# Scaled rotary embedding: the 0/1 matrix built small and repeated by VectorE, fills moved to GpSimd, PSUM copies in pairs

One core of one Trainium2 chip. The metric is the device time of one execution in microseconds (us), the median of several; lower is better. All inputs and the output are in HBM.

## The reference

```python
# x: (8, 8, 1024, 64) float32; freqs: (32,); positions: (1024,); scale = 0.5
angles = np.outer(positions * scale, freqs)
cos, sin = np.cos(angles), np.sin(angles)
x_first, x_second = x[..., :32], x[..., 32:]
out_first  = x_first * cos - x_second * sin
out_second = x_first * sin + x_second * cos
```

The tables depend on the position alone and are shared by the 64 (batch, head) pairs. x and the result are 16.78 MB each.

## The kernel before

Four sets (u = 0 to 3) of 16 heads. A partition holds 128 consecutive positions of one head, so the tables `T` differ between partitions. They are computed once, eight positions per partition (`tab`), and spread by 16 matmuls with a 0/1 matrix `sel`; each result goes from PSUM to the fp16 tile `T` by a copy. GpSimd's queue loads x and converts it to fp16 on the way; half of set 0 comes as fp32 on two other queues and is converted by ScalarE.

```python
    pin(nc.sync.dma_start(out=X0f[:, :Q], in_=xv[0][:, NH : NH + Q]))
    ...                                           # positions, freqs, rest of X0f on ScalarE's queue
    pin(nc.gpsimd.dma_start(out=Xf[0][:, :NH], in_=xv[0][:, :NH]))
    pin(nc.gpsimd.memset(sel, 0.0))               # 128 x 2048
    pin(nc.gpsimd.dma_start(out=Xf[1], in_=xv[1]))
    pin(nc.gpsimd.affine_select(out=sel, ...))    # 128 x 2048
    for u in range(2, NU):
        pin(nc.gpsimd.dma_start(out=Xf[u], in_=xv[u]))
    ...                                           # two fills on VectorE
    pin(nc.vector.tensor_copy(out=posf, in_=...)) # 8 positions, int32 -> fp32 (L98)
    ...                                           # y = posf * cfreq, range reduction, two Sin -> tab
    for g in range(G):                            # 16 matmuls and copies; VectorE has g = 0, 2, 4, 6
        ...
    pin(nc.scalar.copy(out=Xf[0][:, NH:], in_=X0f[:, :NH]))
    for u in range(NU):
        OUT = xout.tile([P, N], FP32, tag="O")
        for s in range(2):
            ...                                   # four VectorE instructions, 7.0 us in all
            pin(nc.scalar.copy(out=OUT[:, ns], in_=Xf[u][:, ns]))      # fp16 -> fp32, 3.6 us
            if u >= NU // 2:
                pin(nc.sync.dma_start(out=ov[u][:, ns], in_=OUT[:, ns]))
        if u < NU // 2:
            pin(nc.gpsimd.dma_start(out=ov[u], in_=OUT))
```

Of the kernel before, what the change touches and what calls it, by code (L numbers as in the profile page):

```python
# [10 lines left out]
FP32 = mybir.dt.float32  # L11
FP16 = mybir.dt.float16
I32 = mybir.dt.int32
AF = mybir.ActivationFunctionType
ALU = mybir.AluOpType
# [6 lines left out]
def kernel(  # L22
# [8 lines left out]
    nc = tc.nc  # L31
    pin = tc.keep_in_program_order
# [3 lines left out]
    half = D // 2  # L36
    P = nc.NUM_PARTITIONS
    HEADS = 16
    HP = P // HEADS
    K = S // HP  # L40
    N = K * D
    NU = NBH // HEADS
    KH = K // 2
    NH = KH * D
    K8 = S // P
    G = P // HP
    W = K8 * half
    assert S % HP == 0 and D == 2 * half and NBH % HEADS == 0 and G * K8 == K

    fscale = float(scale)  # L50

    xv = x.rearrange("b h s d -> (b h s d)").rearrange("(u p n) -> u p n", p=P, n=N)
    ov = out.rearrange("b h s d -> (b h s d)").rearrange("(u p n) -> u p n", p=P, n=N)

    consts = ctx.enter_context(tc.tile_pool(name="consts", bufs=1))
    tmp = ctx.enter_context(tc.tile_pool(name="tmp", bufs=1))
    psum = ctx.enter_context(tc.tile_pool(name="psum", bufs=1, space=bass.MemoryType.PSUM))
    spread = ctx.enter_context(tc.tile_pool(name="spread", bufs=6, space=bass.MemoryType.PSUM))
    xin = ctx.enter_context(tc.tile_pool(name="xin", bufs=1))
    xout = ctx.enter_context(tc.tile_pool(name="xout", bufs=3))  # L60

# [13 lines left out]
    Xf = [t.rearrange("p k h j -> p (k h j)") for t in X]  # L75


    sel = consts.tile([P, G, HEADS, HP], FP16)
    pin(nc.gpsimd.dma_start(out=Xf[0][:, :NH], in_=xv[0][:, :NH]))  # L79
    pin(nc.gpsimd.memset(sel, 0.0))  # L80
    pin(nc.gpsimd.dma_start(out=Xf[1], in_=xv[1]))  # L81
    pin(nc.gpsimd.affine_select(  # L82
        out=sel, in_=sel, compare_op=ALU.not_equal, fill=1.0, base=0,
        pattern=[[-1, G], [0, HEADS], [-G, HP]], channel_multiplier=1,
    ))
    for u in range(2, NU):
        pin(nc.gpsimd.dma_start(out=Xf[u], in_=xv[u]))  # L87


    coef = consts.tile([1, P], FP32)  # L90
    pin(nc.vector.memset(coef, fscale / (2.0 * np.pi)))  # L91
    quarter = consts.tile([P, 1], FP32)
    pin(nc.vector.memset(quarter, np.pi / 2.0))
    cfreq = psum.tile([P, half], FP32)
    nc.tensor.matmul(out=cfreq, lhsT=coef, rhs=freq_row, start=True, stop=True)  # L95

# [2 lines left out]
        out=posf, in_=pos_i64.bitcast(I32).rearrange("p (k t) -> p k t", t=2)[:, :, 0]  # L99
# [3 lines left out]
        out=y,  # L103
# [8 lines left out]
        out=r, in0=m, scalar=_MAGIC, in1=y, op0=ALU.subtract, op1=ALU.subtract  # L112
    ))
    tab = consts.tile([P, 2, K8, half], FP16)
# [3 lines left out]
        out=ra.bitcast(I32), in0=r.bitcast(I32), scalar1=0x7FFFFFFF, scalar2=None, op0=ALU.bitwise_and  # L118
# [2 lines left out]


    T = consts.tile([P, 2, K, half], FP16)
    for g in range(G):
        ps = spread.tile([P, 2, K8, half], FP32, tag="g")
        nc.tensor.matmul(  # L126
            out=ps.rearrange("p t k j -> p (t k j)"),
            lhsT=sel[:, g].rearrange("s h q -> s (h q)"),
            rhs=tab.rearrange("s t k j -> s (t k j)"),
            start=True, stop=True,  # L130
        )
        dst = T[:, :, g * K8 : (g + 1) * K8, :]
        if g % 2 == 0 and g < G // 2:
            pin(nc.vector.tensor_copy(out=dst, in_=ps))  # L134
        else:
            pin(nc.scalar.copy(out=dst, in_=ps))  # L136
# [3 lines left out]
# [3 lines that stand above are left out]
# [9 lines left out]
                out=Xs[:, :, 0, :], in0=Xs[:, :, 0, :], in1=pr[:, :, 1, :], op=ALU.subtract  # L152
            ))
            pin(nc.vector.tensor_tensor(  # L154
                out=Xs[:, :, 1, :], in0=pr[:, :, 0, :], in1=Xs[:, :, 1, :], op=ALU.add
# [41 lines left out]
```

## Time and profile before

| | before |
|---|---|
| time, median of 3 | 85.02 us (84.86 to 85.13) |
| profiled execution | 84.89 us; its profiled span, first to last instruction, 82.7 us |
| VectorE / ScalarE / GpSimd busy | 75% / 49% / 11% |

Head of the page: the span, then busy us, share of the span and number of instructions of each engine.

```profile
span 82.7 us, 185 instructions
PE 6.0 (7%) x18; PEld 2.5 (3%) x18; DVE 62.4 (75%) x43; ACT 40.6 (49%) x24; POOL 9.1 (11%) x12
```

VectorE is the busiest compute engine and the change takes work off it. The four stores on the sync queue (issue duration and first and last start; then the times from issue to landing; the later a store is issued, the shorter its time):

```profile
L159 SPq DMA_DIRECT2D out_dram<-OUT x4: 332/332/342, 53.8 to 75.0; - x4
DMA to landing us min/median/max: 6.8/10.1/13.4
```

The last store is issued at 75.0 us and lands 6.8 us later.

### The profile page before, as it was taken

What the parts mean: (1) busy time and instruction counts of PE and PEld (TensorE: products, weight loads), DVE (VectorE), ACT (ScalarE), POOL (GpSimd) and SP (SyncE); (2) the same over time, 40 slices, a digit from 0 to 9 for tenths busy, and PEclk for the clock granted to TensorE, in tenths of its full rate; (3) what the DMA queues carried; (4) which work ended last, traced back from release to release, by engine and by line L of the source; (5) the groups of instructions that cost most, each with busy time, mean ns of one, the idle gap of its engine ahead of it and who ended that gap; (6) DMA issues with size and microseconds to landing.
All of it is one profiled execution on the core that took longest, in us unless ns stands there. A gap on an engine that the chain in (4) does not pass through costs nothing.

```text
span 82.7 us, 185 instructions
## 1 busy us (share of the span) xinstructions
PE 6.0 (7%) x18; PEld 2.5 (3%) x18; DVE 62.4 (75%) x43; ACT 40.6 (49%) x24; POOL 9.1 (11%) x12
## 2 busy tenths in 40 slices
PE   0011099600000000000000000000000000000000
PEld 0010033100000000000000000000000000000000
DVE  0029657999899999999999999999999999400000
ACT  0600337999993098059219607903940880492000
POOL 4999400000000000200000200000000000000000
PEclk9999999999555555555555555555555555555555
DMA  3899997997998899799989989998999999999991
GB/s 51 327 319 269 301 341 170 254 254 151 230 254 190 190 254 238 158 238 254 127 349 412 507 364 428 475 460 357 420 436 412 428 444 412 452 420 436 436 412 55
DMA packets 1874, 26.22 MB, mean 317 GB/s; under 512 B 338, under 2 KB 338, under 8 KB 338
## 3 DMA queue, kind: packets, MB, share of 16 engines
q0 software_dynamic: 864, 15.73, 66.3%
q1 hardware_dynamic: 720, 9.44, 27.3%
q10 hardware_dynamic: 290, 1.06, 3.2%
HBM read 16.79 MB, written 16.78 MB: 406 GB/s over the span
## 4 chain that ended last, share of the span: by engine, by line
DVE 58%; ACT 15%; DMA 6%; issue 5%; PE 4%; DVEq 1%; ACTq 0%
DVE pr L149 19%; DVE X L150 19%; DVE X L154 9%; DVE X L151 6%; DMA pos_i<-in_positions_dram 6%; ACT T L136 5%; ACT OUT L157 4%; PE ps L126 4%; ACT X L137 4%; DVE posf L98 3%; DVEq L192 1%; DVE r L111 1%; DVE y L102 1%; ACT tab L120 1%; ACT tab L115 1%
## 5 line engine op out<-in xcount | busy, mean ns | idle before, releaser
L157 ACT CAST OUT<-X 128x4096 f32<-128x4096 f16 x8 | 28.9, 3616 | 24.2 <-DVE X L154 24.2
L149 DVE TENSOR_TENSOR pr<-X,T 128x4096 f16<-128x4096 f16 x8 | 18.3, 2292 | 0.9 <-ACT X L137 0.4
L150 DVE TENSOR_TENSOR X<-X,T 128x4096 f16<-128x4096 f16 x8 | 18.3, 2292 | 0.3
L151 DVE TENSOR_TENSOR X<-X,pr 128x2048 f16<-128x2048 f16 x8 | 9.8, 1224 | 0.3
L154 DVE TENSOR_TENSOR X<-pr,X 128x2048 f16<-128x2048 f16 x8 | 9.7, 1218 | 0.0
L136 ACT CAST T<-ps 128x512 f16<-128x512 f32 x12 | 6.3, 621 | 1.9 <-PE ps L126 1.9
L98 DVE CAST posf<-pos_i 128x8 f32<-128x8 int32 x1 | 2.5, 2496 | 4.7 <-DMA pos_i<-in_positions_dram 4.7
L126 PE MATMUL ps<-tab,sel 128*128 128x512 f16 x16 | 5.4, 500 | 4.1 <-ACT tab L120 4.0
L161 POOL DMA_DIRECT2D out_dram<-OUT x2 | 1.1, 534 | 37.3 <-ACT OUT L157 37.3
L134 DVE CAST T<-ps 128x512 f16<-128x512 f32 x4 | 2.8, 691 | 1.7 <-PE ps L126 1.7
L82 POOL TENSOR_SCALAR_AFFINE_SELECT sel<-sel 128x2048 f16<-128x2048 f16 x1 | 3.9, 3865 | 0.1
L137 ACT CAST X<-X0f 128x4096 f16<-128x4096 f32 x1 | 3.7, 3704 | 0.0
L115 ACT ACTIVATE tab<-r 128x256 f16<-128x256 f32 x1 | 0.4, 416 | 6.1 <-DVE r L111 6.1
L115 ACT ACT_TABLE_LOAD x1 | 1.3, 1283 | 2.1 <-issue 2.1
L126 PEld LDWEIGHTS <-sel 128*128 128x128 f16 x16 | 2.0, 122 | 6.9 <-issue 4.3
L80 POOL MEMSET sel<- 128x2048 f16 x1 | 1.8, 1823 | 0.0
L87 POOL DMA_DIRECT2D X<-in_x_dram x2 | 1.1, 554 | 0.0
L95 PE MATMUL cfreq<-freq_row,coef 1*128 1x32 f32 x2 | 0.6, 392 | 5.9 <-DMA freq_row<-in_freqs_dram 5.9
L91 DVE MEMSET coef<- 1x128 f32 x1 | 0.2, 165 | 0.8 <-PEq L178 0.8
L79 POOL DMA_DIRECT2D X<-in_x_dram x1 | 0.7, 667 | 0.8 <-POOLq L178 0.8
L95 PEld LDWEIGHTS cfreq<-freq_row,coef 1*128 1x128 f32 x2 | 0.5, 306 | 5.8 <-issue 5.8
L81 POOL DMA_DIRECT2D X<-in_x_dram x1 | 0.5, 542 | 0.0
(10 smaller groups left out, 2.4 us busy)
## 6 DMA issues: line engine op xcount, KB each, us to landing
out_dram<-OUT POOLq DMA_DIRECT2D x2, 4096.0 KB, 18.7
out_dram<-OUT SPq DMA_DIRECT2D x4, 2048.0 KB, 10.1
X<-in_x_dram POOLq DMA_DIRECT2D x3, 2048.0 KB, 24.1
X0f<-in_x_dram SPq DMA_DIRECT2D x1, 1024.0 KB, 4.8
X<-in_x_dram POOLq DMA_DIRECT2D x1, 1024.0 KB, 11.6
X0f<-in_x_dram ACTq DMA_DIRECT2D x1, 1024.0 KB, 13.1
pos_i<-in_positions_dram ACTq DMA_DIRECT2D x1, 8.0 KB, 4.9
freq_row<-in_freqs_dram ACTq DMA_DIRECT2D x1, 0.1 KB
```

The lines of the kernel that those rows point to most:

```text
L82: pin(nc.gpsimd.affine_select(out=sel, in_=sel, compare_op=ALU.not_equal, fill=1.0, base=0, pattern=[[-1, G], [0, HEADS], [-G, HP]], chann ...
L98: pin(nc.vector.tensor_copy(out=posf, in_=pos_i64.bitcast(I32).rearrange("p (k t) -> p k t", t=2)[:, :, 0]))
L115: pin(nc.scalar.activation(out=tab[:, 0], in_=r, func=AF.Sin, bias=0.0, scale=-_TWO_PI_DN))
L126: nc.tensor.matmul(out=ps.rearrange("p t k j -> p (t k j)"), lhsT=sel[:, g].rearrange("s h q -> s (h q)"), rhs=tab.rearrange("s t k j -> s ...
L134: pin(nc.vector.tensor_copy(out=dst, in_=ps))
L136: pin(nc.scalar.copy(out=dst, in_=ps))
L137: pin(nc.scalar.copy(out=Xf[0][:, NH:], in_=X0f[:, :NH]))
L149: pin(nc.vector.tensor_tensor(out=pr, in0=Xs, in1=sin_b, op=ALU.mult))
L150: pin(nc.vector.tensor_tensor(out=Xs, in0=Xs, in1=cos_b, op=ALU.mult))
L151: pin(nc.vector.tensor_tensor(out=Xs[:, :, 0, :], in0=Xs[:, :, 0, :], in1=pr[:, :, 1, :], op=ALU.subtract))
L154: pin(nc.vector.tensor_tensor(out=Xs[:, :, 1, :], in0=pr[:, :, 0, :], in1=Xs[:, :, 1, :], op=ALU.add))
L157: pin(nc.scalar.copy(out=OUT[:, ns], in_=Xf[u][:, ns]))
```

## The change

Its intent is to relieve VectorE: VectorE's four PSUM copies become two of double size (and ScalarE's twelve become six), two fills go to GpSimd, and GpSimd builds a 128-column matrix in place of 2048 columns, which one VectorE copy repeats.

```diff
--- before.py
+++ after.py
@@ -55,7 +55,7 @@
     consts = ctx.enter_context(tc.tile_pool(name="consts", bufs=1))
     tmp = ctx.enter_context(tc.tile_pool(name="tmp", bufs=1))
     psum = ctx.enter_context(tc.tile_pool(name="psum", bufs=1, space=bass.MemoryType.PSUM))
-    spread = ctx.enter_context(tc.tile_pool(name="spread", bufs=6, space=bass.MemoryType.PSUM))
+    spread = ctx.enter_context(tc.tile_pool(name="spread", bufs=3, space=bass.MemoryType.PSUM))
     xin = ctx.enter_context(tc.tile_pool(name="xin", bufs=1))
     xout = ctx.enter_context(tc.tile_pool(name="xout", bufs=3))
 
@@ -75,22 +75,24 @@
     Xf = [t.rearrange("p k h j -> p (k h j)") for t in X]
 
 
+
+    one = consts.tile([P, G, HP], FP16)
     sel = consts.tile([P, G, HEADS, HP], FP16)
+    coef = consts.tile([1, P], FP32)
+    quarter = consts.tile([P, 1], FP32)
     pin(nc.gpsimd.dma_start(out=Xf[0][:, :NH], in_=xv[0][:, :NH]))
-    pin(nc.gpsimd.memset(sel, 0.0))
-    pin(nc.gpsimd.dma_start(out=Xf[1], in_=xv[1]))
+    pin(nc.gpsimd.memset(coef, fscale / (2.0 * np.pi)))
+    pin(nc.gpsimd.memset(quarter, np.pi / 2.0))
+    pin(nc.gpsimd.memset(one, 0.0))
     pin(nc.gpsimd.affine_select(
-        out=sel, in_=sel, compare_op=ALU.not_equal, fill=1.0, base=0,
-        pattern=[[-1, G], [0, HEADS], [-G, HP]], channel_multiplier=1,
+        out=one, in_=one, compare_op=ALU.not_equal, fill=1.0, base=0,
+        pattern=[[-1, G], [-G, HP]], channel_multiplier=1,
     ))
-    for u in range(2, NU):
+    for u in range(1, NU):
         pin(nc.gpsimd.dma_start(out=Xf[u], in_=xv[u]))
 
 
-    coef = consts.tile([1, P], FP32)
-    pin(nc.vector.memset(coef, fscale / (2.0 * np.pi)))
-    quarter = consts.tile([P, 1], FP32)
-    pin(nc.vector.memset(quarter, np.pi / 2.0))
+    pin(nc.vector.tensor_copy(out=sel, in_=one.unsqueeze(2).broadcast_to((P, G, HEADS, HP))))
     cfreq = psum.tile([P, half], FP32)
     nc.tensor.matmul(out=cfreq, lhsT=coef, rhs=freq_row, start=True, stop=True)
 
@@ -121,16 +123,17 @@
 
 
     T = consts.tile([P, 2, K, half], FP16)
-    for g in range(G):
-        ps = spread.tile([P, 2, K8, half], FP32, tag="g")
-        nc.tensor.matmul(
-            out=ps.rearrange("p t k j -> p (t k j)"),
-            lhsT=sel[:, g].rearrange("s h q -> s (h q)"),
-            rhs=tab.rearrange("s t k j -> s (t k j)"),
-            start=True, stop=True,
-        )
-        dst = T[:, :, g * K8 : (g + 1) * K8, :]
-        if g % 2 == 0 and g < G // 2:
+    for g in range(0, G, 2):
+        ps = spread.tile([P, 2, 2, W], FP32, tag="g")
+        for i in range(2):
+            nc.tensor.matmul(
+                out=ps[:, i].rearrange("p t w -> p (t w)"),
+                lhsT=sel[:, g + i].rearrange("s h q -> s (h q)"),
+                rhs=tab.rearrange("s t k j -> s (t k j)"),
+                start=True, stop=True,
+            )
+        dst = T[:, :, g * K8 : (g + 2) * K8, :].rearrange("p t (i k) j -> p i t (k j)", i=2)
+        if g in (0, 4):
             pin(nc.vector.tensor_copy(out=dst, in_=ps))
         else:
             pin(nc.scalar.copy(out=dst, in_=ps))
```

## The prediction

> **What bounds the kernel now.** I first read section 4 of the page, the chain that ended last, because the change is aimed at VectorE. It names VectorE with 58%, and its pieces in order of time show VectorE running from 14.6 us to 71.3 us with one gap of 0.4 us. That suggests VectorE bounds the kernel. I don't think so, and the reason is in sections 2 and 3 and in the window table.
>
> Section 2 and 3 of the page:
>
> ```profile
> DMA  3899997997998899799989989998999999999991
> q0 software_dynamic: 864, 15.73, 66.3%
> q1 hardware_dynamic: 720, 9.44, 27.3%
> q10 hardware_dynamic: 290, 1.06, 3.2%
> HBM read 16.79 MB, written 16.78 MB: 406 GB/s over the span
> ```
>
> The three queues add up to 96.8% of the time of the 16 DMA engines, and they are busy in the first half (loading x) as well as in the second (storing the result). Nothing is read twice: 8 x 8 x 1024 x 64 floats are 16.78 MB each way, so there is no traffic to save.
>
> Windows cut at the landings (issue time plus time to landing; X1 22.6, X2 32.2; the first half of X0 at 12.9); the last columns are the DMA share and GB/s:
>
> ```profile
> 22.60:32.20 9.60, 0.00 (x0) 0.00 (x0) 9.46 (x6) 5.96 (x2) 0.00 (x0) 0.50 1.02 218
> 42.30:81.00 38.70, 0.00 (x0) 0.00 (x0) 28.61 (x17) 18.03 (x5) 0.53 (x1) 0.50 0.99 428
> 81.00:82.70 1.70, 0.00 (x0) 0.00 (x0) 0.00 (x0) 0.00 (x0) 0.00 (x0) 0.50 0.00 0
> ```
>
> The loads convert fp32 to fp16 and GB/s counts the fp16 bytes, so 218 is 436 GB/s on the HBM side. The stores run from 42.3 to 81.0 at 428 GB/s with share 0.99; 16.78 MB in 38.7 us are 434 GB/s. Both phases run at about the same rate, near 435, and the DMA engines do not pause between them. All stores wait behind the X3 load: the first result (4.19 MB) is issued at 33.0 us, yet by the byte rates its data begins only when X3 is in, at about 42.3.
>
> Does the last store come late enough to set the end? It is issued at 75.0 us (the last ScalarE conversion ends at 74.95). Before it 7 x 2.097 = 14.68 MB are queued; between 42.3 and 75.0, 32.7 x 0.434 = 14.18 MB have gone. So 0.50 MB is left, 1.15 us of work. The first load on that same queue was issued at 0.74 us and its first bytes moved between 1.5 and 2.0, so the issue takes about 1 us to take effect. The backlog just covers this. **Two limits end together**: VectorE's chain feeds the last store just as the DMA queue would have run dry. Making only one of them faster gains almost nothing; making VectorE slower by more than some tenths costs directly.
>
> **What VectorE's start waits for.** The timeline at the start (start, duration):
>
> ```profile
> 4.29 3.87 POOL L82 TENSOR_SCALAR_AFFINE_SELECT sel<-sel 128x2048 f16<-128x2048 f16 x1
> 5.69 2.50 DVE L98 CAST posf<-pos_i 128x8 f32<-128x8 int32 x1 [4.69 <-DMA pos_i<-in_positions_dram]
> 5.86 0.60 PE L95 MATMUL cfreq<-freq_row,coef 1*128 1x32 f32 x2 [5.86 <-DMA freq_row<-in_freqs_dram]
> 8.29 0.42 DVE L102 TENSOR_TENSOR y<-posf,cfreq 128x256 f32<-128x256 f32 x1
> 10.43 5.56 PE L126 MATMUL ps<-tab,sel 128*128 128x512 f16 x16 [3.96 <-ACT tab L120]
> 13.99 4.50 ACT L136 CAST T<-ps 128x512 f16<-128x512 f32 x9 [0.23 <-PE ps L126]
> 14.61 2.29 DVE L149 TENSOR_TENSOR pr<-X,T 128x4096 f16<-128x4096 f16 x1 [0.31 <-ACT T L136]
> ```
>
> A cast of 8 elements takes 2.50 us and ends at 8.19, just after GpSimd's affine_select (8.16). It is not working, it is locked out.
>
> **The Trainium skill.** (1) "SBUF — State Buffer", section "Who interferes with whom": GpSimd and a VectorE copy or cast in a two-port mode take one shared port pair exclusively, and the later one blocks wholly. The pair of lines above agrees (ends 0.03 us apart). (2) "VectorE: DVE Perf Modes", "The perf-mode tier table": a 2048-element 16-bit SBUF copy in 4x mode takes 693 ns, and PSUM sources lose the two-port modes. The trace has no such copy; its PSUM copies (512 fp32, 691 ns) fit one element per cycle plus 151 cycles at that page's 0.96 GHz. (3) "ScalarE: Activation LUTs", "What ACT_TABLE_LOAD costs": 0.833 ns per element plus a fixed part, partly overlapped back to back. The trace agrees: eight copies of 512 from 14.57 to 18.49 are 0.49 us each, 0.43 + 0.06. (4) "DMA: Bandwidth & Descriptors", "Where 436 GB/s comes from": 435.2 GB/s is the ceiling of the 16 ports. The 434 and 436 above agree, so no reserve is left in the DMA rate.
>
> **The change, part by part.**
>
> *Small matrix on GpSimd.* Removed: a fill of 2048 columns (1.82 us) and an affine_select of 2048 (3.87 us). Added: the two fills from VectorE (about 0.1 each, by the 128x1 fills of the trace), a fill of 128 columns (about 0.2) and an affine_select of 128 columns (3.87/16 = 0.24 plus a fixed part that I put at 0.2 to 0.3). The first load's issue ends at 1.93 as before, so the small matrix is there at about 3.0. Then three load issues of 0.55 us, done near 4.7. They now come before 8.1 us, but they queue behind X0, which moves until about 12.9: no byte moves sooner.
>
> *The repeating copy on VectorE.* 0.69 us in 4x mode; runs of 8 elements and the repeated axis could bring it to 1.2 or 2.3 us, both estimates from (2). It starts at 3.0 and ends between 3.7 and 5.3, before the positions land at 5.67. Hidden. TensorE needs the matrix only when tab is there.
>
> *The cast freed.* It starts at 5.69 and takes about 0.16 us, as the 1x128 fill does (0.165). Now y waits for cfreq, which ends at 5.86 + 0.60 = 6.46; with the 0.10 us that lay ahead of y before, y starts at about 6.55 instead of 8.29, **-1.74 us**. From y to the first spread matmul nothing changes (10.43 - 8.29 = 2.14), so that one starts at 8.69.
>
> *Copies in pairs.* The first eight matmuls come 0.43 us apart, and the copies follow them, so here a larger grain costs: the last copy of the first half holds 1024 elements and takes 0.58 + 0.43 = 1.01 us instead of 0.58. It starts as before, 3.56 us after the first matmul. On VectorE 2 x 1.22 = 2.45 replaces 4 x 0.69 = 2.76, all while it waits for TensorE. The three buffers hold: the fourth pair needs the first, free about 2.3 us after the first matmul, and begins at 2.6. So pr starts 4.18 + 0.45 = 4.63 after it: at 13.3 instead of 14.61, **-1.3 us**. X0's first half lands at about 12.9, so the margin there shrinks from 1.7 to 0.4 us. On ScalarE the second half of T takes 4 x 0.92 = 3.7 instead of 3.9; the conversion of X0's second half ends about 1.4 us earlier, near 20.6, and VectorE's first half ends at 13.3 + 7.02 = 20.3. It waits 0.3 instead of 0.4 us. From there VectorE is about 1.4 us ahead.
>
> *Sum on VectorE:* the last multiply chain ends near 69.9 instead of 71.3, the last store is issued near 73.6 instead of 75.0. **Sum at the end:** by 73.6 us 13.58 of the 14.68 MB have gone; 1.10 MB, 2.5 us, is queued ahead of the last store. Its data begins when it did before, at 76.1, and ends at 76.1 + 2.097/0.434 = 80.9. The 1.4 us turn into a longer wait in the queue. I predict **84.8 us** (85.02 before; 0.2 for small gaps near the end that a longer queue may fill).
>
> **Rivals.**
> 1. VectorE's chain sets the end after all, and the 1.4 us come through: 83.6. For it: the chain of section 4. Against it: the stores start only at 42.3, and 16.78 MB need 38.6 us at the rate seen. Even this would be 1.6%.
> 2. The load phase gets shorter, as GpSimd's descriptor work is done early. 16.79 MB took from about 1.7 to 42.3; at 435 GB/s they need 38.6, so 2.0 us are lost there. If all came back: about 83.0. Against it: X1 to X3 were queued before X0 had landed in the kernel before too, so the losses (a dip at 32 to 34 us, the ramp at 2 us) aren't from late issues.
> 3. VectorE starts later than I think: the repeating copy and GpSimd's descriptors lock each other out, X0's first half lands late, or the pairs stall on a buffer. As the last store tolerates only tenths of delay over before, a loss of 1.4 us there eats the gain and no more; a loss of 3 us would give about 86.5. Nothing in the trace points to so much.
>
> **Range and chances.** Full DMA limit 84.8 to 85.1, most of the weight; a part of rival 1 or 2 down to 83.8; jitter up to 85.3. Faster by over 2% means below 83.3, which needs rival 2 nearly whole: 4%. Slower by over 2% means above 86.7: 2%. Within 2%: 94%.
>
> **What would show it.** Right: the cast under 0.3 us; y near 6.5, pr near 13.3; VectorE's last instruction near 70; the last store's issue near 73.6 with its time to landing risen from 6.8 to about 8.2 us; DMA still at 428 GB/s from about 42 us to the end; span 82.5. Wrong: a DMA pause in the second half, stores that begin before 41 us, or a span shortened by as much as VectorE's last end.

## The result

The changed kernel takes **84.53 us** (84.35 to 84.60, 6 runs) against 85.07 us of the kernel before in the same rounds (84.86 to 86.47; the 86.47 is a slow run, and without it the median is 85.02). The ratio is 0.9938, 95% interval 0.9922 to 0.9954: the same within 2%, a small gain clear of noise. Ratios here are the mean time of one kernel's fast runs over that of the other's of the same rounds, so not quite the ratio of the medians quoted.

Head of the page of the changed kernel:

```profile
span 82.8 us, 179 instructions
PE 7.0 (8%) x18; PEld 2.7 (3%) x18; DVE 60.3 (73%) x40; ACT 40.1 (49%) x18; POOL 4.6 (6%) x14
```

GpSimd's busy time is halved, VectorE's is 2.1 us lower, and the span is no shorter: 82.8 against 82.7 us. The start of the changed kernel in order of time (start, duration):

```profile
2.36 0.40 POOL L87 TENSOR_SCALAR_AFFINE_SELECT one<-one 128x128 f16<-128x128 f16 x1
2.71 1.95 POOL L92 DMA_DIRECT2D X<-in_x_dram  x3
2.79 0.69 DVE L95 COPY sel<-one 128x2048 f16<-128x2048 f16 x1 [2.79 <-POOL one L87]
...
5.80 0.17 DVE L100 CAST posf<-pos_i 128x8 f32<-128x8 int32 x1 [2.32 <-DMA pos_i<-in_positions_dram]
6.51 0.42 DVE L104 TENSOR_TENSOR y<-posf,cfreq 128x256 f32<-128x256 f32 x1 [0.53 <-PE cfreq L97]
...
8.70 6.35 PE L129 MATMUL ps<-tab,sel 128*128 128x512 f16 x16 [2.23 <-ACT tab L122]
...
13.36 2.29 DVE L152 TENSOR_TENSOR pr<-X,T 128x4096 f16<-128x4096 f16 x1 [0.67 <-ACT T L139]
```

The cast of the positions takes 0.17 us in place of 2.50; the first spread matmul starts at 8.70 instead of 10.43, the main loop (`pr`) at 13.36 instead of 14.61. From the second half of set 0 on VectorE is 1.5 us ahead (20.52 against 22.02), and this lead is kept to the end of its work. Then the sync queue's stores:

```profile
L162 SPq DMA_DIRECT2D out_dram<-OUT x4: 332/332/342, 52.3 to 73.5; - x4
DMA to landing us min/median/max: 8.4/11.6/14.9
```

The last store is issued 1.5 us earlier and then needs 1.6 us more to land: 73.5 + 8.4 = 81.9, before 75.0 + 6.8 = 81.8. The DMA row in 40 slices, and the window of the stores (the last two columns are DMA share and GB/s):

```profile
DMA  2899998997999899699979989999899999999991
```

```profile
42.30:81.00 38.70, 0.00 (x0) 0.00 (x0) 27.14 (x16) 17.39 (x5) 0.53 (x1) 0.50 1.00 428
```

As before, the DMA engines are busy nearly throughout: between the first and the last slice none is under 0.6. So the span tells one story (the lead is lost in the DMA queue) and the time tells of 0.5 us that the span does not show. Both were tested.

### The profile page after: what moved, and what is told of

It reads as the page before. It is cut to its first block, busy times and chain, and to the rows that moved or that the text cites. A ratio compares the mean times of both kernels' runs of the same rounds, so it can differ in the third digit from the quotient of the medians.

```text
span 82.8 us, 179 instructions
## 1 busy us (share of the span) xinstructions
PE 7.0 (8%) x18; PEld 2.7 (3%) x18; DVE 60.3 (73%) x40; ACT 40.1 (49%) x18; POOL 4.6 (6%) x14
## 3 DMA queue, kind: packets, MB, share of 16 engines
HBM read 16.79 MB, written 16.78 MB: 406 GB/s over the span
## 4 chain that ended last, share of the span: by engine, by line
DVE 55%; ACT 14%; issue 6%; DMA 6%; PE 5%; DVEq 1%; ACTq 0%
DVE pr L152 19%; DVE X L153 19%; DVE X L157 9%; DVE X L154 6%; DMA freq_row<-in_freqs_dram 6%; ACT T L139 5%; ACT OUT L160 4%; PE ps L129 4%; ACT X L140 4%; DVEq L195 1%; PE cfreq L97 1%; ACT tab L122 1%; DVE r L113 1%; DVE y L104 1%; ACTq L69 0%
## 5 line engine op out<-in xcount | busy, mean ns | idle before, releaser
L139 ACT CAST T<-ps 128x1024 f16<-128x1024 f32 x6 | 5.7, 1030 | 2.6 <-PE ps L129 2.6
L129 PE MATMUL ps<-tab,sel 128*128 128x512 f16 x16 | 6.4, 584 | 2.2 <-ACT tab L122 2.2
L137 DVE CAST T<-ps 128x1024 f16<-128x1024 f32 x2 | 2.5, 1225 | 2.2 <-PE ps L129 2.2
L164 POOL DMA_DIRECT2D out_dram<-OUT x2 | 1.1, 536 | 40.3 <-ACT OUT L160 40.3
L95 DVE COPY sel<-one 128x2048 f16<-128x2048 f16 x1 | 0.7, 693 | 2.8 <-POOL one L87 2.8
L100 DVE CAST posf<-pos_i 128x8 f32<-128x8 int32 x1 | 0.2, 172 | 2.3 <-DMA pos_i<-in_positions_dram 2.3
L122 ACT ACTIVATE tab<-ra,quarter 128x256 f16<-128x256 f32 x1 | 0.5, 507 | 0.0
```

The costliest lines, as they stand in the source:

```text
L129: nc.tensor.matmul(out=ps[:, i].rearrange("p t w -> p (t w)"), lhsT=sel[:, g + i].rearrange("s h q -> s (h q)"), rhs=tab.rearrange("s t k ...
L137: pin(nc.vector.tensor_copy(out=dst, in_=ps))
L139: pin(nc.scalar.copy(out=dst, in_=ps))
```

## The experiments

The theory: **two limits**. The end is set by the later of (a) the DMA queue, whose 33.57 MB are through at about 81.9 us, and (b) the last store's issue plus the time that it needs when nothing is ahead of it. The rivals: VectorE's chain alone sets the end; the DMA queue alone does.

### One part of the change at a time

**Fills alone.** `coef` and `quarter` are filled on GpSimd, the rest is as before.

```diff
+    pin(nc.gpsimd.memset(coef, fscale / (2.0 * np.pi)))      # after the first X0 load
+    pin(nc.gpsimd.memset(quarter, np.pi / 2.0))
-    pin(nc.vector.memset(coef, fscale / (2.0 * np.pi)))
-    pin(nc.vector.memset(quarter, np.pi / 2.0))
```

> Only the two fills move from VectorE to GpSimd. My theory (two limits that end together; the DMA queue is the harder one): affine_select starts about 0.2 us later, the locked cast ends about 0.2 to 0.3 us later (8.4 instead of 8.19), the last store is issued 0.2 to 0.3 us later, near 75.3; time 85.0 to 85.3. Separate question: in the changed kernel the time is 0.54 us shorter though the profiled span is not (84.53 against a span of 82.8, before 84.89 against 82.7). If the fills carry what lies outside the span, time minus span is about 1.75 here; if not, it stays near 2.2. Rival (VectorE's chain alone sets the end): the same +0.2 to 0.3, no difference here.

Timeline of this run, affine_select and the cast:

```profile
4.46 3.86 POOL L86 TENSOR_SCALAR_AFFINE_SELECT sel<-sel 128x2048 f16<-128x2048 f16 x1
5.67 2.68 DVE L98 CAST posf<-pos_i 128x8 f32<-128x8 int32 x1 [5.67 <-DMA pos_i<-in_positions_dram]
```

affine_select ends at 8.32 and the cast at 8.35: the cast again ends 0.03 us after it, at another moment. That supports the lock that the prediction describes: VectorE's cast is held back as long as GpSimd's affine_select runs. The last store is issued at 75.2, 0.2 us later, as expected, and the span is 82.8. Yet the time is 84.63 us against 84.97 (ratio 0.9961, 0.9948 to 0.9974), and not the 85.0 to 85.3 expected: faster, though nothing inside the span is.

**Small matrix alone.** The matrix part of the diff; fills on VectorE and single copies as before.

> Only the small matrix and the repeating copy; fills and single copies as before. The cast takes 0.17 us, the first spread matmul starts near 8.7, pr near 12.9 to 13.0 (X0's first half lands at about 12.9 and could hold it), VectorE ends near 69.7, last store issued near 73.3. My theory: the stores end at 81.0 all the same, span 82.6 to 82.8, time 84.4 to 85.0. Rival (VectorE alone sets the end): span 81.0, time 83.3. If the part outside the span comes from here, time minus span is about 1.75.

```profile
8.49 5.24 PE L128 MATMUL ps<-tab,sel 128*128 128x512 f16 x16 [2.17 <-ACT tab L122]
12.93 2.29 DVE L151 TENSOR_TENSOR pr<-X,T 128x4096 f16<-128x4096 f16 x1 [0.76 <-ACT T L138]
```

The stores of the sync queue:

```profile
L161 SPq DMA_DIRECT2D out_dram<-OUT x4: 332/332/342, 51.9 to 73.0; - x4
DMA to landing us min/median/max: 9.0/12.2/15.5
```

With the large affine_select gone the cast takes 0.17 us. The main loop starts 1.7 us earlier than in the kernel before, the last store is issued at 73.0, two full us earlier, and lands after 9.0 us instead of 6.8: at 82.0. Time 84.88 against 84.97 us (ratio 0.9993, 0.9978 to 1.0007). This is the part that speeds VectorE up most, and it gains nothing. The rival by which VectorE alone sets the end is refuted: it asked for 83.3.

**Pairs alone.** The pair loop and `bufs=3`, the rest as before.

> Only the copies in pairs. The cast stays locked (2.5 us). pr starts 0.45 us later than before, near 15.06; ScalarE's conversion of X0's second half ends near 22.1, so VectorE is 0.1 to 0.2 us later from then on, last store issued near 75.15. Theory: the backlog just covers the issue, so +0.0 to +0.2 us: time 85.0 to 85.3. Rival that pairs are a gain by themselves (fewer instructions): pr earlier than 14.6.

```profile
5.71 2.48 DVE L98 CAST posf<-pos_i 128x8 f32<-128x8 int32 x1 [4.71 <-DMA pos_i<-in_positions_dram]
15.07 2.29 DVE L150 TENSOR_TENSOR pr<-X,T 128x4096 f16<-128x4096 f16 x1 [0.67 <-ACT T L137]
```

The cast is locked out as before and `pr` starts at 15.07 instead of 14.61: the coarser copies cost the start of the main loop 0.46 us. The last store is issued at 75.2. The span is 82.8, the time 84.60 us (ratio 0.9956, 0.9943 to 0.9969), again below the kernel before, and below the 85.0 to 85.3 expected, although VectorE is later. So whatever makes this time short is not VectorE's lead.

### Taking the DMA queue out of the way

In this pair of kernels X3 isn't loaded; set 3 is computed from X0's tile. Their outputs are wrong, which doesn't matter for the times. Every engine has the same work, and the DMA engines have 4.19 MB less.

```diff
-    X = [xin.tile([P, K, 2, half], FP16, name=f"X{u}") for u in range(NU)]
+    X = [xin.tile([P, K, 2, half], FP16, name=f"X{u}") for u in range(NU - 1)]
+    X.append(X[0])
-    for u in range(2, NU):          # range(1, NU) in the changed kernel
+    for u in range(2, NU - 1):      # range(1, NU - 1)
         pin(nc.gpsimd.dma_start(out=Xf[u], in_=xv[u]))
```

> The kernel before without the load of X3: the last quarter is computed from X0's tile instead (wrong result on purpose), so every engine does the same work and the DMA queue has 4.19 MB, 9.6 us, less to read. Theory of two limits: loads end near 32.7, the stores begin when they are issued, the queue runs dry, and the last store is alone: issued at 75.0, 1 us to take effect, 4.84 us of data, as before: span 82.5 to 82.8, time 84.7 to 85.0, no gain though a ninth of all bytes is gone, because VectorE's chain ends at the same time. A plain DMA limit without the second one would give 75.

The window from 42 to 52 us (last columns: DMA share, GB/s), in the kernel before and in the cut kernel before:

```profile
42.00:52.00 10.00, 0.00 (x0) 0.00 (x0) 9.86 (x6) 5.39 (x2) 0.53 (x1) 0.50 1.01 436
42.00:52.00 10.00, 0.00 (x0) 0.00 (x0) 9.86 (x7) 5.35 (x2) 0.53 (x1) 0.50 0.59 252
```

The stores of the sync queue in the cut kernel before:

```profile
L160 SPq DMA_DIRECT2D out_dram<-OUT x4: 332/332/342, 53.9 to 75.2; - x4
DMA to landing us min/median/max: 6.2/6.8/9.5
```

The DMA share is 0.59 where it was 1.01 in the kernel before: the queue runs dry. Still the span only falls from 82.7 to 82.3 us (82.7 to 83.0 in the runs of the kernel before beside it; time 84.51, beside it 85.12): one byte in eight of the 33.57 MB is gone (the expectation's "a ninth" is a slip) and 0.4 us of span are gained, because the last store is still issued at 75.2. This refutes the DMA queue as the only limit. The expectation missed by 0.2 us: a store with nothing ahead lands after 6.2 us, not 6.8, so in the kernel before about half a us of the 6.8 was queue.

> The changed kernel with the same cut. Theory: with the queue out of the way the 1.5 us that VectorE gained come through: last store issued at 73.5, landing again after 6.8 us (not 8.4), span 81.1 to 81.3, 1.5 us shorter than the cut kernel before; time near 83.0 to 83.4. Rival (the gain was lost somewhere between VectorE and the end other than in the DMA queue, so the end doesn't follow the last store): span still 82.7.

```profile
L163 SPq DMA_DIRECT2D out_dram<-OUT x4: 332/333/342, 52.0 to 73.3; - x4
DMA to landing us min/median/max: 6.3/6.8/9.5
```

Now the last store, issued at 73.3, lands after 6.3 us as well. The span is 80.5 us, 1.8 us below the cut kernel before, and the issue is 1.9 us earlier: with the queue out of the way VectorE's lead arrives in full. The time is 82.26 us. (The lead is 1.9 and not 1.5 us, in part because this run's first matmul happened to start at 8.40; I had expected a span of 81.1.)

### Making VectorE later

Extra products ahead of the main loop, results unused:

```diff
+    scratch = tmp.tile([P, KH, half], FP16)
+    for _ in range(3):              # 1 or 3 in the changed kernel, 2 in the kernel before
+        pin(nc.vector.tensor_tensor(out=scratch, in0=T[:, 0, :KH], in1=T[:, 0, :KH], op=ALU.mult))
```

> The changed kernel with one extra VectorE product of 1.22 us just before the main loop. VectorE and the last store are about 1.1 us later than in the changed kernel (issue near 74.6). My theory: the queue still holds about 1.1 us of stores then, which covers the 1.0 us that an issue takes; the time is that of the changed kernel, 84.4 to 84.8. Rival (VectorE's chain sets the end): +1.1 us, 85.6.

One product in the changed kernel: the last store is issued at 74.3 instead of 73.5 and lands after 7.5 us, at 81.8. Span 82.7, time 84.77 us (84.50 to 84.96). In the profiled execution the delay is free, as expected. It is the shortest of four, though: their spans are 82.7, 82.9, 83.1 and 83.2, against 82.6 to 82.8 in the changed kernel's six, and the median time is 0.24 us above the changed kernel's. The two come from different rounds, so whether a quarter of a us of the delay does count is not settled.

> The changed kernel with three extra VectorE products (3.7 us) before the main loop; VectorE about 3.6 us later than in the changed kernel, last store issued near 77.1. Theory: the slack of about 1.5 us is used up, the rest counts: last store lands after 6.8 us again, span near 84.8, time 86.5 (2.0 us over the changed kernel). Rival (DMA alone limits, by far): no change. Rival (VectorE alone): +3.6 us, 88.1.

```profile
L166 SPq DMA_DIRECT2D out_dram<-OUT x4: 332/333/342, 55.8 to 76.9; - x4
DMA to landing us min/median/max: 6.3/8.2/11.5
```

Three products: issued at 76.9, landed after 6.3 us, at 83.2. Span 84.1, time 86.11 us. Of 3.5 us of delay 1.3 reach the span; the slack of the changed kernel was about 2.1 us (8.4 - 6.3 to landing). I had expected a span of 84.8, with a slack of 1.5.

> The kernel before with two extra VectorE products (2.45 us) before the main loop; 0.4 us are absorbed by its wait for X0's second half, so VectorE is about 2.0 us later and the last store is issued near 77.0. Theory: the kernel before has nearly no slack (0.1 us), so +1.9 us: span 84.6, time 86.9. If the DMA queue alone set the end of the kernel before, it would stay at 85.0.

```profile
L163 SPq DMA_DIRECT2D out_dram<-OUT x4: 332/332/342, 56.0 to 77.1; - x4
DMA to landing us min/median/max: 6.3/8.1/11.4
```

The kernel before with two products: the last store at 77.1 lands after 6.3 us, span 84.3 (84.6 expected), time 86.07 us (86.9 expected) against 85.12. Of 2.1 us of delay 1.6 arrive, so its slack is about 0.5 us (0.8 if the longest span beside it, 83.0, is taken for 82.7). Put together (issue and landing from the view of the sync queue's stores, as above):

| kernel | last store issued | to landing | landed | span |
|---|---|---|---|---|
| small matrix alone | 73.0 | 9.0 | 82.0 | 82.9 |
| changed | 73.5 | 8.4 | 81.9 | 82.8 |
| changed, one product | 74.3 | 7.5 | 81.8 | 82.7 |
| before | 75.0 | 6.8 | 81.8 | 82.7 |
| changed, three products | 76.9 | 6.3 | 83.2 | 84.1 |
| before, two products | 77.1 | 6.3 | 83.4 | 84.3 |
| before, X3 not loaded | 75.2 | 6.2 | 81.4 | 82.3 |
| changed, X3 not loaded | 73.3 | 6.3 | 79.6 | 80.5 |

With all bytes to move, the last store lands at the later of 81.8 to 82.0 us and its issue + 6.3 us; the span ends 0.9 us after that. One rule holds for all eight rows, and it is the theory of two limits. Its three numbers are read from these same rows, each from one profiled execution, and spans of one kernel in the same rounds mostly differ by 0.1 to 0.3 us, by 0.5 at most; but 6.3 us fits all four rows in which the last store has nothing ahead of it, and in the other six kernels the last store lands at 81.8 to 82.0 too.

### The half microsecond outside the span

The time of the profiled execution minus its span, both as listed with the run, and the number of VectorE instructions against the kernel before, from the edits:

| kernel | VectorE instructions | time | span | difference |
|---|---|---|---|---|
| changed | -3 | 84.53 | 82.8 | 1.7 |
| changed, X3 not loaded | -3 | 82.23 | 80.5 | 1.7 |
| fills alone | -2 | 84.55 | 82.8 | 1.8 |
| pairs alone | -2 | 84.60 | 82.8 | 1.8 |
| changed, one product | -2 | 84.50 | 82.7 | 1.8 |
| before | 0 | 84.89 | 82.7 | 2.2 |
| before, X3 not loaded | 0 | 84.53 | 82.3 | 2.2 |
| changed, three products | 0 | 86.27 | 84.1 | 2.2 |
| small matrix alone | +1 | 85.04 | 82.9 | 2.1 |
| before, two products | +2 | 86.07 | 84.3 | 1.8 |

The difference comes in two sizes, and each kernel shows its own in all its runs (1.73 to 1.82 or 2.12 to 2.24). It isn't the work that the change saves: the kernel before with two more products has the small one. Of the counts by engine in the heads of the pages only VectorE's sorts all ten: 40, 41 and 45 instructions go with the small one, 43 and 44 with the large. It is not a matter of more or fewer. Two kernels were made to test this; each changes nothing but this count, by fills of one column in VectorE's idle time at the start.

```diff
+    pad = consts.tile([P, 1], FP32)
+    for _ in range(2):              # 2 in the kernel before, 3 in the changed one
+        pin(nc.vector.memset(pad, 0.0))
```

> The kernel before plus two fills of one column on VectorE at the start, where it waits for the positions anyway: nothing of the change in it. So far the time minus the profiled span is 2.2 us in the kernel before, in the matrix alone, in the cut kernel before and in the changed kernel with three extra products, and 1.8 us in the changed kernel, fills alone, pairs alone, the cut changed kernel, one extra product, and the kernel before with two extra products. Counted in VectorE instructions against the kernel before that is 0, +1, 0, 0 for 2.2 and -3, -2, -2, -3, -2, +2 for 1.8; no other engine's count sorts them. Theory (the length of VectorE's instruction stream sets what lies outside the span): +2 gives 1.8 here, time 84.5 to 84.65 with the same span of 82.7. Rival (the 0.4 us come from the work that the change saves): time stays 84.9 to 85.1.

```profile
0.81 0.18 DVE L92 MEMSET pad<- 128x1 f32 x2 [0.81 <-PEq L181]
5.70 2.49 DVE L101 CAST posf<-pos_i 128x8 f32<-128x8 int32 x1 [4.57 <-DMA pos_i<-in_positions_dram]
```

The fills are done before 1 us; the cast is locked out as ever and the span is 82.9. The time is 84.66 us against 84.92 (ratio 0.9961, 0.9938 to 0.9984), the difference 1.8 in all four runs. By the ratios two useless instructions bring about 0.33 us (0.14 to 0.53), and the whole change 0.53.

> The changed kernel plus three one-column fills on VectorE ahead of its copy, in idle time. Theory of the stream's length (count 0 against the kernel before): time minus span goes to 2.2, time 84.9 to 85.0, span 82.7 to 82.8, and the measured gain of the change is gone though all its work is there. Rival (the gain belongs to the change's work): 84.5.

```profile
0.81 0.31 DVE L97 MEMSET pad<- 128x1 f32 x3 [0.81 <-PEq L184]
2.79 0.69 DVE L98 COPY sel<-one 128x2048 f16<-128x2048 f16 x1 [1.67 <-POOL one L87]
```

The changed kernel with three useless fills: 85.00 us against 84.92 (ratio 1.0004, 0.9981 to 1.0026), difference 2.2, span 82.8. All the work of the change is there and its gain is gone. What lies behind the count is not shown: the profile begins and ends with the span.

> The change without the pairs. pr near 12.95 (X0's first half lands at 12.9), last store issued near 73.1, span 82.7 to 82.9: the pairs cost VectorE 0.4 us and the end nothing. The count of VectorE instructions is -1 against the kernel before, not seen yet: time 84.5 if it falls to 1.8, 84.9 if to 2.2. A rival by which the pairs are what made the changed kernel faster needs 84.9 and a span longer than 82.8.

The change without pairs (count -1): 84.77 us (ratio 0.9976, 0.9950 to 1.0002), span 82.8, difference 2.05 to 2.10, a size between the two and nearer the large one; the expectation named only 1.8 or 2.2. So pairs or single copies make no difference inside the span. `pr` starts at 13.02 instead of 13.36, yet the last store is issued at 73.4, only 0.1 us before the changed kernel's: the second half of set 0 can't start on VectorE before ScalarE has converted it, and that start is nearly the same (20.43 against 20.52).

### A try at using the slack

All stores on the sync queue in halves, so that they no longer queue behind the load of X3.

```diff
-            if u >= NU // 2:
-                pin(nc.sync.dma_start(out=ov[u][:, ns], in_=OUT[:, ns]))
-        if u < NU // 2:
-            pin(nc.gpsimd.dma_start(out=ov[u], in_=OUT))
+            pin(nc.sync.dma_start(out=ov[u][:, ns], in_=OUT[:, ns]))
```

> The changed kernel with the first two results stored in halves from the sync queue too, so that stores no longer queue behind the X3 load: the first is issued near 24.0 us instead of 31.5, and loads and stores mix. It tries to turn VectorE's slack of about 2 us into time. Theory (the 16 DMA engines are busy from 2 to 81 us and the number of bytes sets the end): no gain from another order, span 82.5 to 83.0, time 84.3 to 84.7, if X3, which now shares the engines with the stores, lands before VectorE needs it at 55.8 us; if it lands later than 57.9, VectorE's slack is used up and the time grows by the rest. Rival (stores waiting behind the load cost time, and the 2 us that the load phase loses against 435 GB/s come back when both kinds mix): span near 81.

Windows of the load phase and the store phase (last columns: DMA share, GB/s), and the landings of X1 to X3:

```profile
2.00:42.30 40.30, 6.95 (x18) 2.76 (x18) 33.17 (x25) 22.75 (x14) 2.56 (x7) 0.69 1.02 263
42.30:81.00 38.70, 0.00 (x0) 0.00 (x0) 27.14 (x16) 17.39 (x5) 0.00 (x0) 0.50 0.99 402
```

```profile
DMA to landing us min/median/max: 19.9/32.0/46.1
```

Stores moved into the first stretch (263 GB/s, with 237 in the kernel before and in the changed one over the same window) and left the second (402 instead of 428). X3 was issued at 4.1 and landed 46.1 us later, at 50.2, in time. The span is 82.9, the time 84.62 us (ratio to the kernel before 0.9952, 0.9925 to 0.9979; difference 1.8): no gain over the changed kernel. With the DMA share at 1.02 and 0.99 in the two stretches, another order of the same bytes ends at the same time. No version that computes the right result beat the changed kernel.

## Why the prediction was right

By its steps:

- **The cast is locked out, not slow**: right. With the small matrix it takes 0.17 us (0.16 predicted); in the fills-alone run it ended 0.03 us after affine_select again.
- **GpSimd's and VectorE's new work**: affine_select of 128 columns took 0.40 us (0.44 to 0.54 predicted), the repeating copy 0.69 us, which is the 4x figure (693 ns) that the Trainium skill gives in "VectorE: DVE Perf Modes", section "The perf-mode tier table". Both are hidden.
- **y at 6.55, matmul at 8.69, pr at 13.3**: measured 6.51, 8.70, 13.36. The pairs cost 0.46 us at pr where 0.45 was worked out.
- **Last store at 73.6, landing after about 8.2 us, span 82.5**: measured 73.5, 8.4 and 82.8. The lead becomes queue time. Shown by the cut pair, in which it arrives in full, and by the delays, of which about 2 us are free.
- **"The DMA engines do not pause between them"** (between loading and storing): not quite. From 38 to 42 us the view gives a DMA share of 0.88 and 147 GB/s in the kernel before, 0.87 and 135 in the changed one, where the loads ran at 218 earlier (fp16 bytes as written). Both kernels have this dip, so it does not touch the forecast.
- **The slack of the kernel before**: mis-sized. The prediction put a backlog of 1.15 us against an issue that takes 1 us, so about 0.15 us of slack. Measured: 6.8 us to landing against 6.3 with nothing ahead, 0.5 us. A store alone is quicker than I took it to be; the error was harmless here and put the spans expected in the two cut kernels and the two longer delays 0.2 to 0.7 us too late.
- **The last 0.2 us**: failed as a reason. I credited "small gaps near the end that a longer queue may fill". The span did not shrink at all. The fall in the median (0.54 us, or 0.49 without the slow run) is the 0.4 us outside the span and a remainder within the spread of the runs; and the 0.4 us go with the count of VectorE instructions, in either direction, not with the work removed. The forecast was a fall of 0.2 us. Without the part outside the span the time would have been about 84.9, in the main part of the range (84.8 to 85.1); with it the 84.53 fell into the part kept for rivals 1 and 2, of which neither came true. That the number comes out so near to 84.8 is luck; that the span hardly changes is not.

What stays open: why the part outside the span depends on that count, and why the load phase moves only 417 GB/s (16.79 MB in the 40.3 us from 2.0 to 42.3, at a DMA share of 1.02), where the stores move 428 by their window. The dip from 38 to 42 us is a part of it; no run tested what causes it.

## What to carry to other kernels

Ask of the last store whether it waits for the engine that feeds it or for the queue ahead of it: compare its time to landing with that of the same store when the queue is empty. Here that gave the slack of each kernel to a few tenths of a us: 0.5 before, 2.1 in the changed kernel. The bytes still queued at the issue, counted from the first profile alone, had told beforehand that 1.5 us saved on the busiest engine would not be seen. And when a fraction of a per cent is gained, check that the profiled span shows it before the edit gets the credit; a control that adds idle-time instructions costs one run.

## What the Trainium skill lacked or had wrong

- No page has it: the time outside the profiled span changed between 1.8 and 2.2 us with the number of VectorE instructions alone (two idle fills more in the kernel before: 84.66 against 84.92 us; three more in the changed kernel: 85.00 against 84.53, the latter from other rounds).
- "DMA: Bandwidth & Descriptors", section "Anatomy of one DMA — SWDGE (gpsimd) path", gives 2.0 us + bytes / 436 GB/s for one transfer, on GpSimd's path; no page has a fit measured on a store from the sync queue. Here 2.097 MB with nothing ahead landed after 6.2 to 6.3 us, so, at the page's rate, the fixed part is by estimate 1.4 to 1.5 us (6.25 - 4.81).
- "GPSIMD Engine Reference" has no durations for the fill and for affine_select. Measured on fp16: fill 1.82 us for 2048 columns and 0.19 for 128; affine_select 3.87 and 0.40.
